# Block weights requested one block ahead, and a quarter of the modulation products moved into the mixers' merge

## The chip, the cores and the metric

The kernel runs on one core of a Trainium2 chip. A core has engines that run beside each other, each with its own instruction stream that it takes strictly in order: TensorE (PE in the profile, its weight loads PEld), VectorE (DVE), ScalarE (ACT), GpSimd (POOL) and SyncE (SP), which here only issues DMAs. They meet at semaphores. The metric is the device time of one execution in microseconds, as the median of the runs.

## The reference, cut to what matters

Two transformer-like layers act on 640 tokens (128 context, 512 latent) of width 1024. The conditioning vectors (one for the context, one for the latents) give nine modulation rows a layer:

```
mods = (silu(cond) @ w_mod[l] + b_mod[l]).reshape(Bc, 9, 1, 1024)
pre(x, s) = rmsnorm(x) * g_pre * (1 + mods[3s+1]) + mods[3s]
f = swiglu(pre(x, 0), w_ffn_gu[l, 0], w_ffn_dn[l, 0]);  x = x + 0.5 * mods[2] * rmsnorm(f) * g_post
m = token_mix(pre(x, 1), ...);                          x = x +       mods[5] * rmsnorm(m) * g_post
f = swiglu(pre(x, 2), w_ffn_gu[l, 1], w_ffn_dn[l, 1]);  x = x + 0.5 * mods[8] * rmsnorm(f) * g_post
swiglu(h) = (silu(h @ Wg) * (h @ Wu)) @ Wd              # 1024 -> 2816 -> 1024
```

`token_mix` ends in a merge: for each of 8 slices c of the width, four branch outputs are multiplied by sigmoid gates `sigmoid(h @ w_gate + b_gate)` and added, and then one projection `w_o` follows. All is float32.

## The kernel before, in words

Tokens lie along the free dimension (two halves of 320 columns), features on the 128 partitions. A float32 operand is split into a rounded part (`wh`, cast by ACT, line 219) and the rest (`wl`, subtracted by DVE, line 220), and each product is three matmuls. Every weight tile thus goes through SP (load into `raw`), ACT and DVE before PE can use it. `advance` does the split some units ahead of use and `fetch` (line 174) issues the loads: it loads until three units of the plan are ahead of the split. The `raw` tiles have three buffers.

Order of work: FFN, mixer, FFN of layer 0, then the same for layer 1. I call the four FFNs FFN1 to FFN4. An FFN's 22 hidden tiles go in four parts of 5, 5, 6 and 6. After each of the first three parts come eight `down` tasks that multiply the part by `w_dn`; POOL adds their results into DRAM (`d_f`, an accumulating DMA). The tiles of parts 1 to 3 (but the last two) are `block` tasks (line 629): a block computes gate and up of one hidden tile with seven half-size products in place of eight, on sums of weights and sums of inputs. Its weights are four pieces of one pair of loads (`raw` for gate, `ru` for up): `b`, `t`, `u` and `4`. The sums are made by three additions on POOL (lines 207 to 209, into the one buffer `wt` and in place into `ru`) when piece `b` is split, and a fourth (line 214) after it. A plan counts each piece as one unit, so `fetch` asks for a block's pair of loads when piece `u` of the block before it is about to be split. There are 15 blocks in each FFN.

The modulation rows are 2 x 9 x 8 = 144 chunks of 128 features. 16 of them are made at the start; the other 128 are made by DVE on the side: a chunk loads 512 KB of `w_mod` (tile `wm`, two buffers, line 340, issued by SP) and takes two products with the conditionings `sc` (line 352), one for each. I call them dots. `room` and `rooms` (line 795) set how many chunks stand in each task of an FFN; `todo` (line 1516) says which FFN makes which rows: 48, 32, 40 and 8 chunks in FFN1 to FFN4. `sc` is kept in DRAM (`d_sc`) and loaded again by each FFN (`cond_silu`). The mixers make none. Engines take their streams in order, so a load that waits in SP's stream holds all loads behind it, and a dot that waits for its `wm` holds DVE's splits behind it.

Of the kernel before, what the change touches and what calls it, by code (L numbers as in the profile page):

```python
# [20 lines left out]
KC = 8  # L21
# [59 lines left out]
class Kernel:  # L81
# [9 lines left out]
    def setup(self):  # L91
        tc, nc, ctx, a = self.tc, self.nc, self.ctx, self.a
        pool = lambda name, bufs, **kw: ctx.enter_context(tc.tile_pool(name=name, bufs=bufs, **kw))
        self.const = pool("const", 1)
        self.slots = pool("slots", 1)
        self.wp = pool("wp", 3)
        self.tp = pool("tp", 4)
        self.psum = pool("psum", 4, space=bass.MemoryType.PSUM)
        self.dram = pool("dram", 1, space=bass.MemoryType.DRAM)

        c = self.const
        self.ones = c.tile([P, P], F32, name="ones")
        nc.vector.memset(self.ones, 1.0)
        self.ident = c.tile([P, P], F32, name="ident")
        make_identity(nc, self.ident)
        self.rsb = c.tile([P, 2], F32, name="rsb")
        for i in range(2):
            nc.vector.memset(self.rsb[:, i:i + 1], (0.5 + 0.5 * i) * LN2 * (127.0 - 0.0430))
        self.eps = c.tile([P, 1], F32, name="eps")
        nc.vector.memset(self.eps, EPS)  # L110
        self.par, self.mod, self.co = [], [], []
        for l in range(DEPTH):
            pt = c.tile([P, C_N], F32, name=f"par{l}")
            nc.scalar.dma_start(pt, a["params"][l])
# [6 lines left out]
        self.d_sc = self.dram.tile([P, 2, D], F32, name="d_sc")  # L121
# [52 lines left out]

    def fetch(self, small):
        st = self.streams[small]
        while st["dma"] < min(st["limit"], st["split"] + (2 if small else 3)):
            ap = st["plan"][st["dma"]]
            if isinstance(ap, Piece):
# [6 lines left out]
                st["raw"].append(ap)  # L186
                st["dma"] += 1
                continue
            r = self.unit_tile(small, ap.shape[-1], F32, "raw")
            self.nc.sync.dma_start(r, ap)  # L190
            st["raw"].append(r)
            st["dma"] += 1

    def make_piece(self, p):
# [8 lines left out]
            self.split(h, lo, g[:, two])  # L203
            return h, lo
        if p.kind == "b":
            t = e["t"] = self.fp.tile([P, 2 * HK], F32, tag="wt", name=self.nm("wt"))
            add(t[:, one], g[:, one], u[:, one])
            add(t[:, two], t[:, one], u[:, two])
            add(u[:, one], u[:, one], u[:, two])
        h = self.unit_tile(False, 2 * HK, F32R, "wh")  # L210
        lo = self.unit_tile(False, 2 * HK, F32R, "wl")
        self.split(h, lo, {"b": g, "t": e["t"], "u": u}[p.kind])
        if p.kind == "b":
            add(g[:, two], g[:, two], e["t"][:, two])
        return h, lo

    def split(self, h, lo, src):

# [104 lines left out]
            pass  # L323


    def cond_silu(self):

        self.sc = self.fp.tile([P, 2, D], F32, tag="sc", name=self.nm("sc"))
        self.nc.sync.dma_start(self.sc, self.d_sc)

    def mods(self, todo, bufs=2):

        nc, a = self.nc, self.a
        loads = []

        def load(i):
            if i < len(todo):
                l, s, c = todo[i]
                wm = self.fp.tile([P, D], F32, tag="wm", name=self.nm("wm"), bufs=bufs)
                nc.sync.dma_start(wm, a["w_mod"][l, s * KC + c])  # L340
                loads.append(wm)

        for i in range(bufs - 1):
            load(i)
        yield
        for i, (l, s, c) in enumerate(todo):
            load(i + bufs - 1)
            wm = loads.pop(0)
            ch = s * KC + c
            for j in range(2):  # L350
                junk = self.t6().bitcast(BF16)[:, :D]
                nc.vector.tensor_tensor_reduce(  # L352
                    junk, wm, self.sc[:, j, :], 0.5, self.par[l][:, C_BMOD + ch:C_BMOD + ch + 1],
                    ALU.mult, ALU.add, self.mod[l][:, ch, j:j + 1])
            if c == KC - 1:
                self.section_done(l, s)
            yield

    def section_done(self, l, s):
        nc = self.nc  # L360
# [205 lines left out]
    def ffn(self, l, st, mod_todo, first=False):  # L566
# [6 lines left out]
        def begin():  # L573
            self.ph = ExitStack()
            self.fp = self.ph.enter_context(self.tc.tile_pool(name=self.nm("ffn"), bufs=1))
            self.side = None
            if mod_todo:
                self.cond_silu()
                self.side = self.mods(mod_todo)
                next(self.side)  # L580
            S["act"] = None
# [211 lines left out]


        room = {"gate": 1.4, "up": 1.4, "down": 1.0, "block": 1.0}
        rooms = [room.get(t.name, 0.0) * (0.5 if t.name == "down" and i < before else 1.0) for i, t in enumerate(mid)]
        done, n = 0.0, 0
        for t, x in zip(mid, rooms):
            done += x
# [17 lines left out]
    def mixer(self, l):  # L817
# [244 lines left out]

        def gate(c, i):
            def fn(w):
                ps = self.ps()
                self.proj(ps, w, KC, self.h)
                G[c, i] = t = self.t6()
                act.activation(two(t), ps[:, :, :HW], AF.Tanh, scale=0.5,
                               bias=self.bg[:, l, i * KC + c:i * KC + c + 1])
# [317 lines left out]
    def build(self):  # L1387
# [6 lines left out]
        def start():  # L1394
# [25 lines left out]
            sc = sp.tile([P, 2, D], F32, name="sc")  # L1420
            pcs = []
            for j in range(2):
                pcs.append(self.ps())
# [77 lines left out]
            def hook(k):  # L1501
# [10 lines left out]
                    hi(k + 2)  # L1512
                if 0 <= k + 1 < KC:
                    lo(k + 1)
                if k == KC - 1:
                    nc.sync.dma_start(self.d_sc, sc)

            hook(-3)
            hook(-2)
            for f in subs:  # L1520
# [2 lines left out]
            self.first_hook = hook  # L1523

        sec = lambda l, r: [(l, s, c) for s in r for c in range(KC)]
        todo = {(0, 0): sec(0, range(2, 8)), (0, 2): sec(0, (8,)) + sec(1, range(0, 3)), (1, 0): sec(1, range(3, 8)),
                (1, 2): sec(1, (8,))}
        nop = lambda: None
        tasks = [Task("start", start)]
        prev = None  # L1530
# [148 lines left out]
```

## Time and profile before

| what | before |
|---|---|
| median of 3 runs | 3316.44 us (3313.45 to 3317.76) |
| profiled execution | 3314.38 us, its span 3312.0 us |
| PE busy | 3069.6 us (93%) |
| DVE busy | 2341.4 us (71%) |
| ACT busy | 1392.3 us (42%) |
| POOL busy | 1092.2 us (33%) |
| DMA | 438.69 MB, 132 GB/s over the span |

The span runs from the first to the last instruction of the program; the 2.4 us to the execution's own time lie outside it. PE is the engine with most work, so time is lost where PE stands idle, and the profile is read by what ended its idle time. "A <- B" means that A's wait was ended by B.

### The profile page before, as it was taken

The numbers are of one execution on the slowest core, as the hardware profiler recorded it, in microseconds if no ns is written. First come the engines' busy times: TensorE is split into PE (matmuls) and PEld (weight loads), VectorE is DVE, ScalarE is ACT, GpSimd is POOL, SyncE is SP. The second block draws the span as 40 slices with busy tenths as digits, with TensorE's granted clock in tenths as the row PEclk, the third lists the DMA queues.
The fourth block names the chain that finished last, engine by engine and source line by source line (L and its number), as shares of the span: only waits on it lengthen the run. The fifth ranks groups of instructions, "written<-read, shape, count | busy, mean of one in ns | idle before, by whom it ended". The sixth has DMA issues, their size and how long they took to land.

```text
span 3312.0 us, 51402 instructions
## 1 busy us (share of the span) xinstructions
PE 3069.6 (93%) x20268; PEld 3001.9 (91%) x20268; DVE 2341.4 (71%) x3336; ACT 1392.3 (42%) x2407; POOL 1092.2 (33%) x856
## 2 busy tenths in 40 slices
PE   7898999899999979989989989988999999899997
PEld 6898988899999979989979889888999999899997
DVE  8877877876653487787787878688666435866666
ACT  4243345444432354343454333454444324543443
POOL 3244244510011243353343352445000113444243
PEclk9899999999999989999999999999999999999999
DMA  5436554411122345436545445533111224434344
GB/s 198 174 131 188 155 181 134 149 58 67 62 83 93 134 146 172 143 122 182 182 156 172 133 154 169 197 122 127 64 64 51 96 90 159 142 136 132 87 132 162
DMA packets 140933, 438.69 MB, mean 132 GB/s; under 512 B 16914, under 2 KB 34130, under 8 KB 139156
## 3 DMA queue, kind: packets, MB, share of 16 engines
q1 hardware_dynamic: 120100, 356.59, 31.5%
q0 software_dynamic: 20304, 78.66, 8.7%
q8 instruction: 159, 2.61, 0.3%
q14 instruction: 82, 0.67, 0.1%
q10 hardware_dynamic: 288, 0.17, 0.0%
HBM read 381.70 MB, written 53.64 MB: 131 GB/s over the span
## 4 chain that ended last, share of the span: by engine, by line
PE 56%; DVE 13%; ACT 4%; issue 3%; DMA 2%; POOL 1%; DVEq 0%; SPq 0%; ACTq 0%; POOLq 0%
PE ps L288 37%; PE ps L642 14%; DVE wl L220 4%; ACT wh L219 1%; PE ps L269 1%; PE ps L271 1%; PE ps L270 1%; DVE slotD L424 1%; DVE t L352 1%; DMA ru<-in_w_gu 1%; DVE slotB L424 1%; DVE W L1211 1%; PE ps L1202 1%; DVE act L220 1%; DMA raw<-in_w_dn 1%
## 5 line engine op out<-in xcount | busy, mean ns | idle before, releaser
L220 DVE TENSOR_TENSOR wl<-raw,wh 128x1024 fp32r<-128x1024 f32 (+3 forms) x525 | 632.0, 1205 | 371.4 <-ACT wh L219 363.1
L288 PE MATMUL ps<-act,wh 128*128 128x320 f32 x2816 | 571.1, 314 | 32.9 <-ACT act L219 19.4
L219 ACT CAST wh<-raw 128x1024 fp32r<-128x1024 f32 (+3 forms) x525 | 481.1, 919 | 153.5 <-PE ps L288 61.1
L642 PE MATMUL ps<-s,wh 128*128 128x320 f32 x1920 | 453.6, 315 | 46.3 <-ACT ps L649 36.6
L288 PEld LDWEIGHTS ps<-act,wh 128*128 128x128 f32 x2816 | 459.7, 191 | 39.3 <-ACT act L219 22.3
L352 DVE CUSTOM_DVE_ANT_0 t<-wm,sc,par 128x1024 bf16<-128x1024 f32 x256 | 373.4, 1495 | 24.4 <-DMA wm<-in_w_mod 24.0
L642 PEld LDWEIGHTS ps<-s,wh 128*128 128x128 f32 x1920 | 329.2, 189 | 63.7 <-ACT ps L649 52.3
L288 PE MATMUL ps<-slotA,wh 128*128 128x320 f32 x1312 | 366.4, 317 | 13.7 <-ACT wh L219 11.2
L288 PE MATMUL ps<-slotA,wl 128*128 128x320 f32 x1312 | 363.1, 314 | 7.2 <-DVE wl L220 7.0
L288 PE MATMUL ps<-slotD,wh 128*128 128x320 f32 x1312 | 352.9, 317 | 15.4 <-DVE slotD L1490 12.6
L288 PE MATMUL ps<-slotB,wh 128*128 128x320 f32 x1312 | 362.0, 314 | 3.1 <-DVE slotB L481 1.6
L288 PE MATMUL ps<-slotC,wh 128*128 128x320 f32 x1312 | 353.1, 317 | 7.4 <-ACT wh L219 3.1
L288 PE MATMUL ps<-act,wl 128*128 128x320 f32 x1408 | 356.6, 312 | 3.3 <-DVE wl L220 3.3
L642 PE MATMUL ps<-s,wl 128*128 128x320 f32 x960 | 298.8, 311 | 2.1 <-DVE wl L220 2.1
L288 PEld LDWEIGHTS ps<-slotA,wh 128*128 128x128 f32 x1312 | 238.8, 192 | 16.8 <-ACT wh L219 12.2
L288 PEld LDWEIGHTS ps<-slotD,wh 128*128 128x128 f32 x1312 | 236.9, 193 | 18.3 <-DVE slotD L1490 14.0
L288 PEld LDWEIGHTS ps<-act,wl 128*128 128x128 f32 x1408 | 248.7, 192 | 4.1 <-DVE wl L220 3.8
L288 PEld LDWEIGHTS ps<-slotA,wl 128*128 128x128 f32 x1312 | 239.0, 192 | 11.3 <-DVE wl L220 10.2
L288 PEld LDWEIGHTS ps<-slotC,wh 128*128 128x128 f32 x1312 | 237.1, 193 | 9.5 <-ACT wh L219 3.4
L288 PEld LDWEIGHTS ps<-slotB,wh 128*128 128x128 f32 x1312 | 238.9, 192 | 4.4 <-DVE slotB L481 2.2
L288 PE MATMUL ps<-slotC,wl 128*128 128x320 f32 x960 | 240.2, 316 | 2.0 <-DVE wl L220 1.8
L778 ACT COPY s<-ps 128x640 f32<-128x640 f32 x96 | 66.6, 694 | 298.6 <-issue 169.2
(340 smaller groups left out, 6466.0 us busy)
## 6 DMA issues: line engine op xcount, KB each, us to landing
raw<-in_w_gu SPq DMA_DIRECT2D x162, 512.0 KB, 4.2
wm<-in_w_mod SPq DMA_DIRECT2D x144, 512.0 KB, 4.3
raw<-in_w_dn SPq DMA_DIRECT2D x96, 384.0 KB, 3.3
raw<-in_w_gate SPq DMA_DIRECT2D x64, 512.0 KB, 3.5
d_f<-s POOLq DMA_DIRECT2D x96, 320.0 KB, 4.9
ru<-in_w_gu SPq DMA_DIRECT2D x60, 512.0 KB, 5.2
raw<-in_w_in SPq DMA_DIRECT2D x44, 512.0 KB, 3.4
raw<-in_w_dn SPq DMA_DIRECT2D x64, 320.0 KB, 2.9
```

The source lines that it names most:

```text
L219: self.nc.scalar.copy(h, src)
L220: self.nc.vector.tensor_sub(lo, src, h.bitcast(F32))
L269: nc.tensor.matmul(out, sh, mh, start=(k == 0), stop=False)
L270: nc.tensor.matmul(out, sh, ml, start=False, stop=False)
L271: nc.tensor.matmul(out, sl, mh, start=False, stop=(k == n - 1))
L288: nc.tensor.matmul(ps[:, hf, :HW], st[:, ws], m[:, k0 + k, hf * HW:(hf + 1) * HW], start=(first and k == 0 and i == 0), stop=(last and k = ...
L352: nc.vector.tensor_tensor_reduce(junk, wm, self.sc[:, j, :], 0.5, self.par[l][:, C_BMOD + ch:C_BMOD + ch + 1], ALU.mult, ALU.add, self.mod ...
L424: nc.vector.scalar_tensor_tensor(x, t, gain, x, op0=ALU.mult, op1=ALU.add)
L642: nc.tensor.matmul(o, w[x][:, ws], a[y][:, k, :], start=(new and k == 0 and i == 0), stop=(k == n - 1 and i == 2), skip_group_check=not new)
L778: nc.scalar.copy(t.rearrange("p (a b) -> p a b", a=2), ps[:, :, :HW])
L1202: nc.tensor.transpose(pv[:, o:o + P], pt[qi][:, j * P:(j + 1) * P], self.ident)
L1211: dve.tensor_sub(lo, src, h.bitcast(F32))
```

## The change

1. `fetch` no longer counts pieces. It counts `raw` tiles held (at most three) and up-weights in waiting (at most two), so that a block's pair of loads is issued as soon as the pair before the last has been split. The three additions are a function `sums`, called for the next block after piece `u`.
2. The chunks of modulation rows 6 and 7 (those of the second FFN of a layer) move from the FFNs into the mixer of the same layer: in the merge, each `gate(c, 1)` and `gate(c, 2)` loads one chunk into one new buffer `self.wm` ahead of its projection and places its two dots behind it. That is 16 chunks a mixer. The FFNs keep 32, 28, 28 and 8.
3. `sc` stays on chip; the four loads of 1 MB and the store go. `wm` in the FFNs has three buffers in place of two.
4. The chip memory for it comes from the DMA descriptor ring of POOL, which is given 4096 bytes a partition.

```
 def fetch(self, small):
-    while st["dma"] < min(st["limit"], st["split"] + (2 if small else 3)):
+    while st["dma"] < st["limit"]:
         ap = st["plan"][st["dma"]]
+        piece = isinstance(ap, Piece)
+        held = sum(not isinstance(r, Piece) or r.kind == "4" for r in st["raw"])
+        if not (piece and ap.kind != "b"):
+            if held >= (2 if small else 3):
+                return
+            if piece and sum(isinstance(r, Piece) and r.kind == "u" for r in st["raw"]) >= 2:
+                return
...
 def make_piece(self, p):
         if p.kind == "b":
-            t = e["t"] = self.fp.tile([P, 2 * HK], F32, tag="wt", name=self.nm("wt"))
-            add(t[:, one], g[:, one], u[:, one])
-            add(t[:, two], t[:, one], u[:, two])
-            add(u[:, one], u[:, one], u[:, two])
+            self.sums(p)
...
+        if p.kind == "u":
+            for q in self.streams[False]["raw"]:
+                if isinstance(q, Piece) and q.kind == "b":
+                    self.sums(q)
...
-    def mods(self, todo, bufs=2):
+    def mods(self, todo, bufs=3):
...
         def gate(c, i):
             def fn(w):
+                todo = [(l, 6 + i - 1, c)] if i in (1, 2) else []
+                for t in todo:
+                    self.load_mod(self.wm, *t)
                 ps = self.ps()
                 self.proj(ps, w, KC, self.h)
+                for t in todo:
+                    self.dots(self.wm, *t)
...
-        todo = {(0, 0): sec(0, range(2, 8)), (0, 2): sec(0, (8,)) + sec(1, range(0, 3)), (1, 0): sec(1, range(3, 8)),
-                (1, 2): sec(1, (8,))}
+        todo = {(0, 0): sec(0, range(2, 6)), (0, 2): sec(0, (8,)) + sec(1, (0, 1)) + half[:4],
+                (1, 0): half[4:] + sec(1, range(3, 6)), (1, 2): sec(1, (8,))}
...
-    nc = _bacc.Bacc("TRN2", target_bir_lowering=False, num_devices=1)
+    nc = _bacc.Bacc("TRN2", target_bir_lowering=False, num_devices=1,
+                     dynamic_dma_scratch_size=4096)
```

PE's and ACT's streams are the same instruction for instruction. Three places show what moves on the others. First SP's stream where part 2 of FFN2 begins: `raw` and `ru` with `in_w_gu` are a block's pair, `in_w_dn` is a down weight, `wm` a chunk. Before:

```order
355 L340 DMA wm_13379<-in_w_mod 128x1024
356 L190 DMA raw_13385<-in_w_dn 128x640
357 L340 DMA wm_13425<-in_w_mod 128x1024
358 L184 DMA raw_13431<-in_w_gu 128x1024
359 L185 DMA ru_13432<-in_w_gu 128x1024
360 L340 DMA wm_13473<-in_w_mod 128x1024
361 L340 DMA wm_13517<-in_w_mod 128x1024
362 L340 DMA wm_13566<-in_w_mod 128x1024
363 L340 DMA wm_13610<-in_w_mod 128x1024
364 L184 DMA raw_13616<-in_w_gu 128x1024
365 L185 DMA ru_13617<-in_w_gu 128x1024
```

and of the change:

```order
351 L367 DMA wm_13348<-in_w_mod 128x1024
352 L199 DMA raw_13354<-in_w_dn 128x640
353 L367 DMA wm_13394<-in_w_mod 128x1024
354 L194 DMA raw_13400<-in_w_gu 128x1024
355 L195 DMA ru_13401<-in_w_gu 128x1024
356 L194 DMA raw_13442<-in_w_gu 128x1024
357 L195 DMA ru_13443<-in_w_gu 128x1024
358 L367 DMA wm_13484<-in_w_mod 128x1024
359 L367 DMA wm_13533<-in_w_mod 128x1024
360 L367 DMA wm_13577<-in_w_mod 128x1024
361 L194 DMA raw_13591<-in_w_gu 128x1024
```

The second block's pair stood behind four chunk loads; it now stands ahead of them.

Second, DVE's stream at the start of the merge of layer 0 (`ps` to `sa` is the spatial gating's output, `br` its split, `swl` a branch weight's split, the ISA rows with `wm` are dots). Before:

```order
1040 L220 TENSOR_TENSOR wl_9279<-raw_9060,wh_9278 128x1024
1041 L1340 SCALAR_TENSOR_TENSOR sa_5560<-ps_9288,par_86,t_1365_9282 64x512
...
1053 L220 TENSOR_TENSOR br_9329<-sa_5560,br_9328 128x640
1054 L220 TENSOR_TENSOR wl_9340<-raw_9219,wh_9339 128x1024
1055 L220 TENSOR_TENSOR swl_9403<-sraw_8913,swh_9402 128x256
1056 L1083 SCALAR_TENSOR_TENSOR t_1361_9274<-t_1361_9274,ps_9406 128x640
```

and of the change:

```order
975 L373 ISA t_1312_9174,mod_88<-wm,sc,par_86 128x1024
977 L373 ISA t_1313_9176,mod_88<-wm,sc,par_86 128x1024
979 L243 TENSOR_TENSOR wl_9183<-raw_8959,wh_9182 128x1024
980 L1364 SCALAR_TENSOR_TENSOR sa_5459<-ps_9192,par_86,t_1318_9186 64x512
...
992 L243 TENSOR_TENSOR br_9233<-sa_5459,br_9232 128x640
993 L243 TENSOR_TENSOR wl_9244<-raw_9118,wh_9243 128x1024
994 L373 ISA t_1328_9297,mod_88<-wm,sc,par_86 128x1024
996 L373 ISA t_1329_9299,mod_88<-wm,sc,par_86 128x1024
998 L243 TENSOR_TENSOR swl_9312<-sraw_8812,swh_9311 128x256
999 L1107 SCALAR_TENSOR_TENSOR t_1314_9178<-t_1314_9178,ps_9315 128x640
```

Two dots stand ahead of the spatial gating's output, and two more between its split and that of a branch weight.

Third, POOL's stream around the same part 2 of FFN2 (the additions of the first and second block). Before:

```order
320 L209 TENSOR_TENSOR ru_13432<-ru_13432 128x512
321 L214 TENSOR_TENSOR raw_13431<-raw_13431,wt_13523 128x512
322 L782 DMA d_f<-s_1990_13563 128x640
323 L782 DMA d_f<-s_1997_13607 128x640
324 L207 TENSOR_TENSOR wt_13687<-raw_13616,ru_13617 128x512
```

and of the change:

```order
320 L238 TENSOR_TENSOR ru_13401<-ru_13401 128x512
321 L220 TENSOR_TENSOR raw_13400<-raw_13400,wt_13490 128x512
322 L801 DMA d_f<-s_1966_13530 128x640
323 L801 DMA d_f<-s_1973_13574 128x640
324 L236 TENSOR_TENSOR wt_13587<-raw_13442,ru_13443 128x512
```

The call of `sums` has moved in the code, but nothing has moved in POOL's stream.

## Rows read from the trace of the kernel before

**Rows 1.** The page's head and PE's line: busy us, share, instructions.

```profile
span 3312.0 us, 51402 instructions
PE 3069.6 (93%) x20268; PEld 3001.9 (91%) x20268; DVE 2341.4 (71%) x3336; ACT 1392.3 (42%) x2407; POOL 1092.2 (33%) x856
```

**Rows 2.** Windows: first down to last block of FFN1 to FFN4, busy by engine.

```profile
core 0: us, PE busy (x) PEld busy (x) DVE busy (x) ACT busy (x) POOL busy (x), PEclk, DMA share, GB/s
128.20:476.00 347.80, 311.29 (x2022) 302.78 (x2021) 275.50 (x366) 129.26 (x203) 137.53 (x87) 0.97 0.49 155
1269.90:1594.30 324.40, 306.22 (x2020) 299.37 (x2019) 249.03 (x329) 128.99 (x203) 130.73 (x86) 0.99 0.49 153
1767.50:2110.10 342.60, 310.21 (x2018) 302.08 (x2017) 266.54 (x359) 129.00 (x203) 131.64 (x86) 0.98 0.50 157
2904.50:3219.20 314.70, 301.58 (x2022) 296.33 (x2021) 192.22 (x233) 129.37 (x203) 121.29 (x87) 1.00 0.40 118
```

**Rows 3.** The same stretches, DVE's line 352 alone: four instructions a chunk.

```profile
128.20:476.00 347.80, 117.88 (x159) 0.97 0.49 155
1269.90:1594.30 324.40, 90.44 (x127) 0.99 0.49 153
1767.50:2110.10 342.60, 115.52 (x157) 0.98 0.50 157
2904.50:3219.20 314.70, 25.11 (x32) 1.00 0.40 118
```

**Rows 4.** Who waited for whom: us in total, times, longest us; SPq is SP's queue.

```profile
SPq L340 <- DVE mod L352: 539.4, 92, 14.7
POOL wt L207 <- DMA ru<-in_w_gu: 64.5, 8, 9.8
POOL wt L207 <- DVE wl L220: 43.9, 28, 3.2
DVE t L352 <- DMA wm<-in_w_mod: 24.0, 16, 3.8
```

**Rows 5.** Windows: FFN2's downs before part 2, its part 2, and FFN4's part 2.

```profile
1377.30:1412.50 35.20, 35.20 (x241) 35.15 (x241) 28.07 (x38) 11.78 (x17) 11.76 (x10) 1.00 0.83 228
1412.50:1499.40 86.90, 78.49 (x507) 75.63 (x506) 68.52 (x90) 36.25 (x59) 40.17 (x23) 0.98 0.37 123
3044.60:3124.20 79.60, 75.85 (x507) 74.01 (x506) 56.51 (x70) 36.44 (x59) 35.22 (x23) 1.00 0.27 82
```

**Rows 6.** Timelines at that start of part 2: start us, us, instruction, idle before.

```profile
1396.20 19.09 SPq L340 DMA_DIRECT2D wm<-in_w_mod  x4
1415.39 0.42 SPq L184 DMA_DIRECT2D raw<-in_w_gu  x1
1424.01 1.04 ACT L219 CAST wh<-raw 128x1024 fp32r<-128x1024 f32 x1 [3.78 <-DMA raw<-in_w_gu]
1426.77 0.41 PE L642 MATMUL ps<-s,wh 128*128 128x320 f32 x1 [3.48 <-DVE t L659]
```

**Rows 7.** Window: the merge of layer 0 from its second gate to the last branch.

```profile
966.00:1117.00 151.00, 151.00 (x1030) 150.78 (x1030) 59.36 (x82) 40.94 (x63) 19.39 (x9) 1.00 0.32 105
```

**Rows 8.** Line 352: duration ns min/median/max of the 256 dots, first and last start.

```profile
L352 DVE CUSTOM_DVE_ANT_0 t<-wm,sc,par x256: 1269/1280/2650, 86.9 to 3192.4; 128x1024 bf16<-128x1024 f32 x128
```

**Rows 9.** Timelines of DVE and PE at the start of that merge.

```profile
964.22 1.23 DVE L220 TENSOR_TENSOR wl<-raw,wh 128x1024 fp32r<-128x1024 f32 x1 [1.17 <-ACT wh L219]
965.37 4.15 DVE L1340 SCALAR_TENSOR_TENSOR sa<-ps,par,t 64x512 f32<-64x512 f32 x8
975.68 0.42 DVE L220 TENSOR_TENSOR swl<-sraw,swh 128x256 fp32r<-128x256 f32 x1
974.87 0.45 PE L288 MATMUL ps<-W,swh 128*128 128x320 f32 x2
```

**Rows 10.** POOL's timeline behind FFN2's last block, and landing of the chunk loads.

```profile
1608.05 0.54 POOL L600 DMA_DIRECT2D slotC<-d_f  x1 [4.22 <-DMA slotD<-d_x]
wm<-in_w_mod SPq DMA_DIRECT2D x144, 512.0 KB, 4.3
```

More of the change, by code (lines that the diff above doesn't have):

```diff
@@ L120, in setup @@
             nc.vector.tensor_scalar_mul(self.bg[:, l, :], self.par[l][:, C_BGATE:C_BGATE + 32], 0.5)
-        self.d_sc = self.dram.tile([P, 2, D], F32, name="d_sc")
+        self.sc = c.tile([P, 2, D], F32, name="sc")
+        self.wm = c.tile([P, D], F32, name="wm")
         self.d_x = self.dram.tile([P, KC, T], F32, name="d_x")
@@ L176, in fetch @@
         st = self.streams[small]
-        while st["dma"] < min(st["limit"], st["split"] + (2 if small else 3)):
+        while st["dma"] < st["limit"]:
             ap = st["plan"][st["dma"]]
-            if isinstance(ap, Piece):
+            piece = isinstance(ap, Piece)
[5 more added lines that the diff above has]
+                    return
+            if piece:
                 if ap.kind == "b":
@@ L185, in fetch @@
                     self.nc.sync.dma_start(e["u"], ap.up)
[L186 to L190, printed above, removed]
+                r = ap
+            else:
+                r = self.unit_tile(small, ap.shape[-1], F32, "raw")
+                self.nc.sync.dma_start(r, ap)
             st["raw"].append(r)
@@ L214, in make_piece, with sums @@
             add(g[:, two], g[:, two], e["t"][:, two])
+        if p.kind == "u":
+            for q in self.streams[False]["raw"]:
+                if isinstance(q, Piece) and q.kind == "b":
+                    self.sums(q)
         return h, lo
+    def sums(self, p):
+        e = p.env
+        if "t" in e:
+            return
+        g, u = e["g"], e["u"]
+        one, two = slice(0, HK), slice(HK, 2 * HK)
+        add = self.nc.gpsimd.tensor_add
+        t = e["t"] = self.fp.tile([P, 2 * HK], F32, tag="wt", name=self.nm("wt"))
+        add(t[:, one], g[:, one], u[:, one])
+        add(t[:, two], t[:, one], u[:, two])
+        add(u[:, one], u[:, one], u[:, two])
     def split(self, h, lo, src):
@@ L323, in rms_r @@
             pass
-    def cond_silu(self):
-        self.sc = self.fp.tile([P, 2, D], F32, tag="sc", name=self.nm("sc"))
-        self.nc.sync.dma_start(self.sc, self.d_sc)
-    def mods(self, todo, bufs=2):
-        nc, a = self.nc, self.a
+    def mods(self, todo, bufs=3):
         loads = []
@@ L337, in load @@
             if i < len(todo):
[L338 to L341, printed above, removed]
+                loads.append(self.fp.tile([P, D], F32, tag="wm", name=self.nm("wm"), bufs=bufs))
+                self.load_mod(loads[-1], *todo[i])
         for i in range(bufs - 1):
@@ L345, in mods, with load_mod, dots @@
         yield
-        for i, (l, s, c) in enumerate(todo):
+        for i, t in enumerate(todo):
             load(i + bufs - 1)
[L348 to L356, printed above, removed]
-            yield
+            self.dots(loads.pop(0), *t)
+            yield
+    def load_mod(self, wm, l, s, c):
+        self.nc.sync.dma_start(wm, self.a["w_mod"][l, s * KC + c])
+    def dots(self, wm, l, s, c):
+        ch = s * KC + c
+        for j in range(2):
+            junk = self.t6().bitcast(BF16)[:, :D]
+            self.nc.vector.tensor_tensor_reduce(
+                junk, wm, self.sc[:, j, :], 0.5, self.par[l][:, C_BMOD + ch:C_BMOD + ch + 1],
+                ALU.mult, ALU.add, self.mod[l][:, ch, j:j + 1])
+        if c == KC - 1:
+            self.section_done(l, s)
     def section_done(self, l, s):
@@ L577, in begin @@
             if mod_todo:
-                self.cond_silu()
                 self.side = self.mods(mod_todo)
@@ L795, in ffn @@
         room = {"gate": 1.4, "up": 1.4, "down": 1.0, "block": 1.0}
-        rooms = [room.get(t.name, 0.0) * (0.5 if t.name == "down" and i < before else 1.0) for i, t in enumerate(mid)]
+        rooms = [room.get(t.name, 0.0) * (0.3 if t.name == "down" and i < before else 1.0) for i, t in enumerate(mid)]
         done, n = 0.0, 0
@@ L1419, in start @@
             nc.vector.tensor_mul(cf, cf, th)
-            sc = sp.tile([P, 2, D], F32, name="sc")
+            sc = self.sc
             pcs = []
@@ L1514, in hook @@
                     lo(k + 1)
-                if k == KC - 1:
-                    nc.sync.dma_start(self.d_sc, sc)
             hook(-3)
@@ L1525, in build @@
         sec = lambda l, r: [(l, s, c) for s in r for c in range(KC)]
-        todo = {(0, 0): sec(0, range(2, 8)), (0, 2): sec(0, (8,)) + sec(1, range(0, 3)), (1, 0): sec(1, range(3, 8)),
-                (1, 2): sec(1, (8,))}
+        half = sec(1, (2,))
+        todo = {(0, 0): sec(0, range(2, 6)), (0, 2): sec(0, (8,)) + sec(1, (0, 1)) + half[:4],
+                (1, 0): half[4:] + sec(1, range(3, 6)), (1, 2): sec(1, (8,))}
         nop = lambda: None
```

## The prediction

> **What bounds the kernel now.** I read the page first. PE has 3069.6 us of work in a span of 3312.0 [rows 1], so 242 us at most can be won by filling its gaps, and DVE, ACT and POOL have less to do. The question is in which stage the gaps are and what DVE has to do there. So next I took windows of the same stretch of all four FFNs, from the first down matmul to the end of the last block [rows 2]. PE has the same work in each of them (some 2020 matmuls), ACT too, yet they last 347.8, 324.4, 342.6 and 314.7 us. What differs is DVE: 275.5, 249.0, 266.5 and 192.2 us busy. The same windows for line 352 alone say why [rows 3]: 159, 127, 157 and 32 instructions. A dot is two instructions and a chunk two dots, so the stretches hold 40, 32, 40 and 8 chunks. The side work that DVE does for the modulation is what stretches an FFN, and not in proportion. From 8 to 32 chunks it costs 9.7 us, 0.40 us a chunk. From 32 to 40 it costs 18.2 us in FFN3 (2.3 a chunk) and 23.4 in FFN1 (2.9).
>
> The waits and the timelines say how. A chunk load has two buffers and can be issued only when a dot has freed one: SP stands 539.4 us on that [rows 4], and what is behind it in its stream stands too. At the start of part 2 of FFN2, four chunk loads hold SP for 19.09 us up to 1415.3, and the second block's pair is issued only then [rows 6]. The rest is a chain: ACT idles 3.78 us for that `raw` and starts the cast at 1424.01, DVE's split and then its line 659 come late behind ACT, and PE idles 3.48 us until 1426.77 [rows 6]. POOL waits at line 207 for `ru`, 8 times and 64.5 us in all [rows 4]. Part 2 of FFN2 takes 86.9 us where that of FFN4, with hardly a chunk, takes 79.6 [rows 5].
>
> **The change part by part.** *Fewer chunks in the FFNs.* 16 go from each layer: FFN1 has 32, FFN2 28, FFN3 28, FFN4 8. Of FFN1's 48, 40 fell in the stretch of rows 3 and 8 before it, where the plan had put 11: DVE lagged by three. The new plan puts 7 of 32 before it, so 25 to 28 fall in the stretch; I take 26. By 314.7 + 0.40 x (chunks - 8), FFN1's stretch becomes 322.0 (gain 25.8), FFN2's and FFN3's 322.8 (gains 1.6 and 19.8), and FFN4's stays. That is 47.2 us. The least: FFN1 and FFN3 only come down to FFN2's 324.4, 41.6 us less what a plan in other places may cost. The most: all three come down to FFN4's 314.7, 33.1 + 9.7 + 27.9 = 70.7 us, which nothing in this profile allows to exceed.
>
> *Pairs requested earlier.* In SP's new order the second block's pair stands ahead of the chunk loads. So the case of rows 6 goes: FFN2's part 2 may lose its 7.3 us over FFN4's [rows 5]. Then FFN2's point of the line is no longer 324.4 but 317.1, 0.10 us a chunk, and the three FFNs gain up to 6 us more each, 18 in all. Zero is the other end, if the pair then waits for a buffer or the engines of the DMA. I take the middle, 9 us.
>
> *The additions called earlier.* I cost this at nothing. POOL's stream is the same before and after, so they can only start earlier if what they wait for comes earlier. In steady state that is the one buffer `wt`, freed by a DVE split (28 waits [rows 4]), and that stays. The 8 waits for `ru` belong to the pair loads, counted above.
>
> *Three `wm` buffers, `sc` kept.* The third buffer lets a chunk load go out one chunk earlier; it is a part of what makes the line hold, and I count no more for it. The four 1 MB loads stand where FFNs begin, beside the heads; no wait of PE names them: zero.
>
> *The dots in the merge.* A merge has 16 chunks, 32 dots. A dot takes 1.28 us in the median, up to 2.65 beside a POOL instruction [rows 8], so 41 us of DVE by the median in 151 us, where DVE is busy 59.4 and PE never idles [rows 7]. PE runs a gate in 48 matmuls and a branch in 12 or 24; at 151.0 / 1030 = 0.147 us each, a gate and its branch take 8.8 or 10.6 us, and DVE has 59.36 / 16 = 3.7 us of work there. Two dots fit, and the weights that DVE splits there are needed a gate later. The exception is the start. The first two dots stand ahead of the split at 964.22, before which DVE idled 1.17 us [rows 9]: 2.56 less 1.17, so the spatial gating's output, begun at 965.37, comes up to 1.4 us late; PE stands right behind it. The next two stand ahead of the split that ended at 976.10, and PE needs that weight 12 matmuls after 974.87, at 976.63 [rows 9]: 0.5 us of slack for 1.4 + 2.56. So PE loses about 3.5 us a merge, 7 us for two. Bounds: nothing, if half of it hides in DVE's idle time; 5.5 us a merge if the second two run beside POOL at 2.3 us.
>
> *The smaller ring.* POOL's transfers are already held to a number in flight: behind FFN2's last block POOL issues eight loads of `d_f`, one of `d_x` and eight of `d_f`, and the last of these waits 4.22 us for the landing of the `d_x`, eight before it [rows 10]; its data is wanted only in the second half of the tail. I cost the ring at zero, with up to 10 us at the high end should it hold POOL sooner.
>
> The Trainium skill, "SBUF — State Buffer", section "SBUF size: 192, 224, or 256?", books 16 KiB a partition for the descriptors of POOL's DMAs; it gives no price for less, and no row of before shows the ring full. If a quarter of the ring meant a quarter of the transfers in flight, two in place of eight, the sum would move toward the high end of the range and no further.
>
> The sum: 47.2 + 9 - 7 = 49 us. The profiled execution took 3314.4 us, 2.4 of them outside the span, which stay: 3265 us. It lies 2.1 us under the median of the three runs, so I set the time at 3267 us.
>
> **The rivals.** *A, the loads collide.* Nothing is loaded less in the downs: the second pair, 1 MB, now falls into a stretch where the DMA engines are busy 0.83 of the time [rows 5], ahead of three chunk loads. DVE then waits for its chunks, and as it goes in order, the next block's splits wait with it. For it: DVE waits for chunk loads already, 16 times and up to 3.8 us [rows 4]. Against it: with three buffers a load has two downs to land in, not one. If each of the nine part starts in FFN1 to FFN3 loses such a 3.8 us, 34 us go back: 3301 us.
>
> On this the Trainium skill speaks against the change: "DMA: Bandwidth & Descriptors", section "Issuing engines are not separate DMA queues", has all DMAs run on the same 16 engines and interleave, so a load brought forward slows the others. The trace does not contradict it; by that rule alone the result would be rival A's.
>
> *B, the merge pays it back.* The slower side. In the merge there is one `wm` buffer: a load can go out only after the last chunk's dots, and DVE stands until it lands. A chunk load lands 4.3 us after its issue [rows 10]. If half of the 32 chunks show PE that landing and the dots, 6.9 us, the price is 110 us, the sum 3316 - 56 + 110 = 3370 us. It decides from 56 / 32 = 1.75 us a chunk. Against it: the free 4 to 6 us in each pair, and that a load goes out most of a pair ahead of its dots.
>
> *C, the FFNs lose all their stretch.* With pairs in time, chunks cost nothing below DVE's limit: 70.7 us from above and no loss in the merge: 3246 us. Against it: FFN4 has 8 chunks, these have 26 to 28.
>
> **How the numbers follow.** My forecast has 0.66 (3253 to 3282), A 0.16, B 0.08, C 0.10. The range reaches from C to A, 3246 to 3301. Faster, by over 0.2% (about what a measurement of this kernel can tell, 6.6 us), are my case, C and most of A: 0.88. A might end within 0.2% at 0.04. Slower is B: 0.08.
>
> **What would show it.** In the changed profile the stretches of rows 2 should be near 322 for the first three, with 26 to 28 chunks; POOL's wait for `ru` under 15 us, the second pair issued before the downs end, and no PE idle of 3.5 us at the start of a part. The merge should last 154 to 155 us in place of 151, with one wait of PE on `br` or `swl` at its start and none later. Waits of DVE for `wm` over 24 us in the FFNs speak for A; waits of PE in the middle of the merge for B. I am wrong if the stretches of FFN1 and FFN3 stay above 330 with the chunks gone: then DVE's load is not what stretches them.

## The result, and the profile after

The changed kernel takes 3268.4 us (median; 3263.9 to 3271.4) beside 3317.1 us (3313.5 to 3322.4) of the kernel before on the same chip: 0.9851 of it, with a 95% interval of 0.9833 to 0.9869. The prediction was 3267 us.

The page's head and PE's line, which answer to [rows 1]:

```profile
span 3269.4 us, 51367 instructions
PE 3057.0 (94%) x20268; PEld 2990.7 (91%) x20268; DVE 2364.8 (72%) x3336; ACT 1392.4 (43%) x2407; POOL 1088.8 (33%) x856
```

The span is 42.6 us shorter (the profiled execution was the longest of its four, 3271.4 us). No engine has less to do to speak of; PE's gaps went from 242 to 212 us, and its own time fell by 12.6 us, at the same number of matmuls. Of PE's waits, the one for ACT's copy of a result in a block (line 652 before, 671 now) fell most, from 27.1 to 10.4 us:

```profile
PE ps L642 <- ACT t L652: 27.1, 28, 3.3
PE ps L661 <- ACT t L671: 10.4, 23, 1.1
```

Where the time went is seen in the four stretches of [rows 2] and their dots [rows 3] (windows of the changed kernel: us, busy by engine with instructions, then clock, DMA share, GB/s):

```profile
130.23:451.94 321.71, 304.77 (x2022) 298.20 (x2021) 235.90 (x301) 126.74 (x199) 131.23 (x87) 0.99 0.47 142
1247.84:1567.75 319.91, 304.57 (x2022) 297.80 (x2021) 244.41 (x313) 128.81 (x203) 133.10 (x86) 0.99 0.48 147
1742.12:2062.07 319.95, 303.11 (x2022) 296.19 (x2021) 245.72 (x314) 128.76 (x203) 132.24 (x86) 1.00 0.48 147
2858.93:3174.67 315.74, 302.97 (x2022) 297.78 (x2021) 195.57 (x233) 129.66 (x203) 120.96 (x86) 0.99 0.41 116
```

and the dots alone (DVE's line 373, which was 352):

```profile
130.23:451.94 321.71, 75.07 (x103) 0.99 0.47 142
1247.84:1567.75 319.91, 82.59 (x111) 0.99 0.48 147
```

The stretches became 26.1, 4.5 and 22.7 us shorter and FFN4's 1.0 longer, 52.2 in all. They hold 26, 28 and 28 chunks (103 and 111 instructions, four a chunk). Outside them the span grew by 9.6 us. The waits that answer to [rows 4] (who waited for whom: us, times, longest):

```profile
SPq L367 <- DVE mod L373: 157.0, 46, 8.8
POOL wt L236 <- DVE wl L243: 49.6, 36, 1.7
DVE t L373 <- DMA wm<-in_w_mod: 11.2, 10, 2.4
```

SP stands 157 us for a dot in place of 539; POOL's wait for `ru` is no longer listed; DVE waits less for chunks, not more. The start of FFN2's part 2, which answers to [rows 6], in SP's queue:

```profile
1375.64 0.33 SPq L194 DMA_DIRECT2D raw<-in_w_gu  x1
1376.02 0.50 SPq L195 DMA_DIRECT2D ru<-in_w_gu  x1
1376.57 14.74 SPq L367 DMA_DIRECT2D wm<-in_w_mod  x3
```

The second block's pair goes out at 1375.64, 15 us before the part begins at 1390.8; it was 2.9 us after it. The chunk loads still hold SP for 14.74 us, but behind the pair. PE's longest wait in that part is now this one (it was 3.48 us):

```profile
1402.14 0.41 PE L661 MATMUL ps<-s,wh 128*128 128x320 f32 x1 [1.27 <-DVE t L678]
```

In each merge, which answers to [rows 7, 9], PE now waits twice, both at the start (the first merge; DVE's and PE's timelines):

```profile
938.81 1.28 DVE L373 CUSTOM_DVE_ANT_0 t<-wm,sc,par 128x1024 bf16<-128x1024 f32 x1
941.15 4.13 DVE L1364 SCALAR_TENSOR_TENSOR sa<-ps,par,t 64x512 f32<-64x512 f32 x8
952.65 1.28 DVE L373 CUSTOM_DVE_ANT_0 t<-wm,sc,par 128x1024 bf16<-128x1024 f32 x1
953.86 0.42 DVE L243 TENSOR_TENSOR swl<-sraw,swh 128x256 fp32r<-128x256 f32 x1
949.37 0.56 PE L311 MATMUL ps<-br,swh 128*128 128x320 f32 x2 [0.81 <-ACT br L242]
954.34 0.56 PE L311 MATMUL ps<-W,swl 128*128 128x320 f32 x2 [1.49 <-DVE swl L243]
```

The dots at 938.81 delay the spatial gating's output, and the split `br` comes 0.81 us late; the next two delay the split of the branch weight by 1.49 us. No wait of PE stands behind the other 28 dots of the merge.

### The profile page after: what moved, and what is told of

Its sections match the earlier page's. It is cut to its first block, busy times and chain, and to the rows that moved or that the text cites. A ratio compares the mean times of both kernels' runs of the same rounds, so it can differ in the third digit from the quotient of the medians.

```text
span 3269.4 us, 51367 instructions
## 1 busy us (share of the span) xinstructions
PE 3057.0 (94%) x20268; PEld 2990.7 (91%) x20268; DVE 2364.8 (72%) x3336; ACT 1392.4 (43%) x2407; POOL 1088.8 (33%) x856
## 5 line engine op out<-in xcount | busy, mean ns | idle before, releaser
L243 DVE TENSOR_TENSOR wl<-raw,wh 128x1024 fp32r<-128x1024 f32 (+3 forms) x525 | 645.5, 1232 | 421.2 <-ACT wh L242 413.0
L373 DVE CUSTOM_DVE_ANT_0 t<-wm,sc,par 128x1024 bf16<-128x1024 f32 x256 | 374.4, 1498 | 11.3 <-DMA wm<-in_w_mod 11.2
```

The lines of the kernel that those rows point to most:

```text
L243: self.nc.vector.tensor_sub(lo, src, h.bitcast(F32))
L373: self.nc.vector.tensor_tensor_reduce(junk, wm, self.sc[:, j, :], 0.5, self.par[l][:, C_BMOD + ch:C_BMOD + ch + 1], ALU.mult, ALU.add, sel ...
```

## The experiments

All times were taken beside the kernel before on the same chip. The table has the ratio to it with its 95% interval, and the four stretches, from windows of one profiled execution as in [rows 2].

| kernel | time us | ratio | FFN1 | FFN2 | FFN3 | FFN4 |
|---|---|---|---|---|---|---|
| before | 3317 | 1 | 347.8 | 324.4 | 342.6 | 314.7 |
| the change | 3268.4 | 0.9851 (0.9833 to 0.9869) | 321.7 | 319.9 | 320.0 | 315.7 |
| chunks moved, pairs as before | 3271.7 | 0.9863 (0.9843 to 0.9882) | 320.0 | 321.8 | 323.8 | 315.2 |
| pairs earlier, chunks as before | 3301.4 | 0.9954 (0.9938 to 0.9969) | 339.3 | 321.9 | 336.3 | 314.5 |
| additions not called earlier | 3269.2 | 0.9853 (0.9837 to 0.9870) | 321.2 | 319.8 | 319.5 | 315.4 |
| small ring alone | 3318.9 | 1.0007 (0.9997 to 1.0017) | 349.9 | 325.8 | 340.6 | 316.1 |
| two `wm` buffers | 3269.4 | 0.9853 (0.9840 to 0.9867) | 321.4 | 320.2 | 322.0 | 315.6 |
| merge's first dots moved | 3262.9 | 0.9828 (0.9814 to 0.9841) | 321.3 | 320.0 | 320.5 | 315.6 |
| 28 more chunks in the fills | 3272.7 | 0.9857 (0.9844 to 0.9871) | 317.9 | 317.5 | 321.3 | 312.2 |
| 20 more, in quiet gates | 3261.1 | 0.9828 (0.9815 to 0.9842) | 318.0 | 320.1 | 321.4 | 316.2 |
| thin dots | 3237.5 | 0.9750 (0.9736 to 0.9764) | 309.1 | 313.5 | 312.3 | 313.7 |
| one load an FFN | 3267.1 | 0.9838 (0.9825 to 0.9852) | 321.3 | 320.0 | 320.5 | 315.5 |
| before with one load | 3291.6 | 0.9920 (0.9906 to 0.9933) | 334.9 | 319.6 | 333.6 | 316.1 |
| before with thin dots | 3236.1 | 0.9756 (0.9743 to 0.9769) | 311.7 | 314.3 | 316.3 | 313.6 |

The kernel before and the one with the small ring alone run the same instructions, and their stretches differ by 2.1, 1.4, 2.0 and 1.4 us. A difference of up to 2 us in a single stretch tells nothing by itself.

### The chunks without the pairs, and the pairs without the chunks

The first has the new `todo`, the dots in the merge, `sc` kept and the small ring, but the old `fetch`, the old additions and two `wm` buffers. The second is the other part alone:

```
 first:   + gate: self.load_mod(self.wm, *t) ... self.dots(self.wm, *t);  new todo, rooms;  sc kept
 second:  + fetch counts held raw tiles and up-weights;  sums() called after piece u
```

> The chunks move into the merge, sc stays on chip and the ring is small, but pairs are requested as before and wm keeps two buffers. My theory (the chunk count is what stretches the FFNs): the stretches of FFN1 to FFN3 fall to about 322, 323 and 323 us, the merges lose 2.6 us each, the whole gains 40 us, ratio 0.988. Rival (late pairs are what stretches them, the chunks only happen to be there): the pairs stay late, at most 20 us are gained, ratio 0.994 or more.

> Only the request of the pairs and the place of the call of the additions change; chunks, buffers, sc and ring are those of before. My theory: a gain of 9 to 18 us (ratio 0.9946 to 0.9973), FFN1 and FFN3 stay above 335 us with their 40 chunks. Rival (late pairs are the cause): 30 us or more, ratio 0.991 or less, and all three stretches near 322. Rival (loads collide): no gain or a loss, with more waits of DVE for wm.

Both theories held: chunks alone gave 45.5 us (40 expected), pairs alone 15.8 (9 to 18), and FFN1 and FFN3 stayed above 335 us in the second. Together they gave 48.7 us, not 61. With the chunks moved, the pairs are worth some 3 us (3271.7 to 3268.4), and the intervals of the two ratios overlap. Why, is seen in the first kernel at the start of FFN2's part 2 (SP's queue and PE's wait):

```profile
1371.49 16.40 SPq L346 DMA_DIRECT2D wm<-in_w_mod  x3
1387.94 0.42 SPq L186 DMA_DIRECT2D raw<-in_w_gu  x1
1398.03 0.42 PE L640 MATMUL ps<-s,wh 128*128 128x320 f32 x1 [0.58 <-DVE t L657]
```

The second pair is still held behind chunk loads, and is issued 0.6 us after its part began (at 1387.37, by the first matmul of line 640). But PE then loses 0.58 us, where it lost 3.48 at 2.9 us [rows 6]. With three chunk loads in the queue in place of four the pair came 2.3 us sooner, and that was nearly enough.

### The additions, the ring, the third buffer

```
 additions:  - if p.kind == "u": ... self.sums(q)      (from the changed kernel)
 ring:       + dynamic_dma_scratch_size=4096           (to the kernel before)
 buffers:    - def mods(self, todo, bufs=3)   + bufs=2 (in the changed kernel)
```

> The changed kernel, with the three additions called only at piece b as before. The streams of all five engines are the same as in the changed kernel. My theory: the same time as the changed kernel, ratio to before 0.985. Rival (the earlier call matters, by the semaphores it waits on): 5 us or more slower than the changed kernel, ratio 0.987 or more.

> The kernel before with a ring of 4096 bytes a partition and nothing else. My theory: no difference, ratio 0.999 to 1.001, and POOL's loads behind a last block issue at the same intervals. Rival (the small ring holds POOL's DMAs back): 3 to 10 us slower, ratio 1.001 to 1.003, with longer waits of POOL behind the last blocks.

> The changed kernel with two wm buffers in the FFNs, as before the change, in place of three. Theory: with 28 chunks an FFN and the pairs ahead of them, SyncE waits for a dot but nothing that it holds is late, so the third buffer is worth nothing: within 4 us of the changed kernel, 0.984 to 0.986 of before. Rival: the third buffer is what lets a load land in time; without it VectorE waits at every part's start, some 4 us nine times: 3290 to 3305 us, 0.992 or more.

None of the three can be told from its neighbour (0.9853, 1.0007, 0.9853). With the additions called early or late, all engines run the same instructions in the same order. The ring's smaller size costs at most 0.2%. With two buffers the three chunk loads at FFN2's part 2 hold SP 14.27 us in place of 14.74, behind the pair as before.

### The start of the merge

```
-todo = [(l, 6 + i - 1, c)] if i in (1, 2) else []
+todo = [(l, 6 + i - 1, c)] if i in (1, 2) and c else []
+if c == KC - 1 and i in (0, 3):
+    todo = [(l, 6 if i == 0 else 7, 0)]
```

> The changed kernel with the four dots at the start of each merge (chunk 0 of rows 6 and 7) moved to the last two gates of the fill ahead of it, where the tensor engine never stood and VectorE was busy 52 of 90 us. Theory: the 2.6 us a merge that the changed kernel loses at its first gate (1.0 us on br, 1.65 us on swl) come only from those four dots, so both merges lose nothing there: about 5 us less than the changed kernel, 3263 to 3264 us, 0.983 to 0.984 of before. Rival: the loss is handed on to the next branch or comes back in the fill: 3268 us, 0.985.

No wait of PE is left in the window of the merge. The two mixers (from FFN1's stretch to FFN2's, and from FFN3's to FFN4's) are 3.6 and 3.2 us shorter than in the changed kernel, and all that lies outside the stretches sums to 1982.7 us, as before the change (1982.5; 1992.1 in the changed kernel). So the theory holds: the four dots were the loss. By the median this version is 5.5 us faster than the changed kernel (3262.9 and 3268.4 us), though the intervals of the two ratios overlap.

### Dots or loads

Two kernels take the two halves of a chunk apart. In thin dots, the FFNs' dots run over one column in place of 1024, all loads stay; with one load, an FFN's dots all run on its first `wm`.

```
 thin dots:  - junk, wm, self.sc[:, j, :], 0.5     + junk[:, :1], wm[:, :1], self.sc[:, j, :1], 0.5
 one load:   - if i < len(todo): load              + if i < 1: load
```

> The changed kernel with the FFNs' dots taken over one column in place of 1024 (their sums are left out); loads, waits and instruction order stay. VectorE has about 70 us less to do in each of FFN1 to FFN3. Theory: what the chunks still cost in an FFN is VectorE's time, so the first three stretches (321.7, 320.1, 320.0 us) come down to FFN4's 315.7 or below, by 0.22 us a chunk: 15 to 25 us less than the changed kernel, 3244 to 3254 us, 0.978 to 0.981 of before. Rival: it is the transfers of the chunks and the places of their loads in SyncE's stream; then at most 3 us go, 3265 us or more, 0.984 or more.

> The counterpart: the changed kernel with one chunk load an FFN and all of the FFN's dots on that one tile (the rows made in the FFNs are then wrong in value); the dots keep their number, place and length, 92 loads of 512 KB and their waits are gone. Theory (VectorE's time): within 3 us of the changed kernel, 3265 to 3271 us, 0.984 to 0.986. Rival (transfers and the loads' place): the 15 to 25 us go here, 0.978 to 0.981.

Without DVE's time 33 us go (0.9851 to 0.9750), more than I expected; without 48 MB of loads nothing goes that can be told (0.9851 to 0.9838). What the chunks still cost is the time of their dots, not their loads. With thin dots POOL's instructions are shorter too (33.55 us in place of 40.32 in the windows below), and no run tells POOL's share from DVE's. Where, is seen by setting the downs before FFN2's part 2 and that part beside each other. The changed kernel:

```profile
1355.60:1390.80 35.20, 35.20 (x243) 35.20 (x241) 26.85 (x37) 11.77 (x17) 11.80 (x10) 1.00 0.84 243
1390.80:1473.10 82.30, 76.44 (x505) 73.81 (x504) 69.69 (x88) 36.15 (x59) 40.32 (x23) 1.00 0.37 117
```

and with thin dots:

```profile
1337.00:1372.20 35.20, 35.20 (x242) 35.20 (x241) 15.35 (x39) 11.77 (x17) 11.73 (x10) 1.00 0.89 251
1372.27:1451.00 78.73, 75.37 (x505) 73.79 (x504) 54.49 (x87) 36.65 (x59) 33.55 (x23) 1.00 0.38 119
```

The eight downs take 35.20 us with six chunks' dots at full length or over one column: there chunks are free. The same holds for the second and third eight downs of all four FFNs in these two kernels (35.20 and 42.24 us). The part's six blocks take 82.3 or 78.7: chunks cost where they stand in blocks. One such place, in the second block of that part, step by step (timelines of DVE, ACT and PE of the changed kernel):

```profile
1404.12 1.27 DVE L373 CUSTOM_DVE_ANT_0 t<-wm,sc,par 128x1024 bf16<-128x1024 f32 x1
1405.32 2.30 DVE L373 CUSTOM_DVE_ANT_0 t<-wm,sc,par 128x1024 bf16<-128x1024 f32 x1
1410.27 1.07 DVE L690 TENSOR_TENSOR t<-t,t 128x320 f32<-128x320 f32 x1
1411.37 0.73 ACT L242 CAST act<-t 128x640 fp32r<-128x640 f32 x1 [3.24 <-DVE t L690]
1412.00 0.42 ACT L671 COPY t<-ps 128x320 f32<-128x320 f32 x1
1412.47 0.42 PE L661 MATMUL ps<-slotA,wh 128*128 128x320 f32 x1 [0.49 <-ACT t L671]
```

The two dots (the second beside an addition of POOL, 2.30 us) push the block's last product on DVE, line 690, back; ACT's cast of it waits 3.24 us, and behind that cast in ACT's stream stands the copy of line 671, for which PE waits. Over the kernel PE waits 23 times and 10.4 us for that copy; with thin dots that wait is not listed. It is half of the 21 us by which PE's gaps shrink with thin dots (from 212.4 to 191.4 us); PE's own time falls by another 16.6 us (3057.0 to 3040.4) at the same number of matmuls.

The same two cuts in the kernel before:

> The kernel before the change with one chunk load an FFN and all of the FFN's dots on that tile (the rows made in the FFNs are wrong in value): no chunk load holds SyncE's queue any more, and VectorE keeps all 48, 32, 40 and 8 chunks. Theory (VectorE's time is most of what the chunks cost, the held loads the smaller part, as the earlier pairs alone gave 16 us): 12 to 20 us less than before, 0.994 to 0.996, and FFN1 and FFN3 still near 340 and 337 us. Rival (what stretches FFN1 and FFN3 from 32 to 40 chunks is SyncE held by chunk loads): 40 us or more go, 0.988 or less.

> The kernel before the change with the FFNs' dots taken over one column in place of 1024 (their sums are left out); all loads and all places stay. Theory (VectorE's time): FFN1 to FFN3 come down to 312 to 318 us, some 70 to 80 us less than before, 0.976 to 0.979. Rival (the place of the loads in SyncE's queue counts by itself, and dots shorter by 1.2 us free a buffer only that much sooner): a part's first block stays late, 25 us or more of it remain, 0.983 or more.

Without the dots' time the kernel before is as fast as the changed kernel without it (3236.1 and 3237.5 us), with all its chunk loads and the old order of the pairs: the theory. The cut is not quite clean, since shorter dots also free the buffers sooner: four chunk loads still hold SP for 17.15 us at FFN2's part 2, but the second pair goes out 1.4 us ahead of the part, where it was 2.9 us behind its start. Without the held loads 25 us went, more than I expected of it and less than the rival wanted. The two causes overlap: the two gains, 80.7 and 25.2 us, cannot be added. That a late pair costs most where DVE has no room to catch up would explain it, but no run shows this by itself.

### Still fewer chunks in the FFNs

The mixer places its `gate(c, 0)` and `gate(c, 3)` between the steps of the attention; these stretches are the fills.

```
 28 more:  gate(c, 0) and gate(c, 3), c < 7: one chunk each of rows 5 and (1, 0) or (1, 8)
 20 more:  gate(c, 3), c < 7, and gate(c, 0), c = 1, 3, 5 alone; both with the merge's first dots moved
```

> A version meant to beat both: as the one before, and 28 more chunks (14 a mixer) moved out of the FFNs into the fill gates of the attention, one a gate, two dots behind each projection. FFN1 to FFN4 keep 26, 20, 22 and 0 chunks in place of 32, 28, 28 and 8. Theory: the remaining slope, 0.22 us a chunk between 8 and 28 chunks, times 28 is 6 us off the FFNs, and the fills take the dots for nothing, as VectorE was busy 60 to 64% of them and the tensor engine over 99%: 3256 to 3259 us, 0.982. Rival: in the fills a dot of 1.28 us stands ahead of a softmax step for which ScalarE and then the tensor engine wait; 28 chunks at 0.5 us or more pay it all back: 3268 us or more, 0.985 or more.

> The version with 28 more chunks in the fills, cut to 20: none in the gates at which that one lost time (the first, where VectorE's stream was full, 3.4 us late on swl and 2.8 on br; and the third, fifth and seventh of the first kind, where dots stood ahead of the splits of the attention's weights, line 1239, 1.3 to 1.5 us each). FFN1 to FFN4 keep 25, 23, 23 and 5 chunks. Theory: those places alone cost the 17 us that its two mixers lost, the other gates are free, and the FFNs give back 0.3 us a chunk, as the thin dots showed (28 us for 92 chunks): 6 us less than the version with the merge's start alone, 0.980 to 0.9815 of before. Rival: the dots in the quiet gates also come back, as later softmax steps or a lower clock: 0.983 or more.

The first fell to its rival. Its FFNs gave back 8.5 us, but its mixers took more. PE's waits in the first mixer's fills (who waited for whom: us, times, longest):

```profile
PE ps L292 <- DVE W L1239: 3.6, 3, 1.3
PE ps L311 <- DVE swl L243: 3.0, 1, 3.0
PE ps L311 <- ACT br L242: 2.6, 1, 2.6
```

and DVE at the first of the three waits for `W`:

```profile
728.07 1.28 DVE L373 CUSTOM_DVE_ANT_0 t<-wm,sc,par 128x1024 bf16<-128x1024 f32 x1
729.27 1.28 DVE L373 CUSTOM_DVE_ANT_0 t<-wm,sc,par 128x1024 bf16<-128x1024 f32 x1
730.60 1.55 DVE L1239 TENSOR_TENSOR W<-ps,W 128x768 fp32r<-128x768 f32 x2
```

DVE had room in the fill (62 of 80 us busy), but not at that gate. The second version left those four gates of a mixer out, and none of the three waits grew there: the quiet gates are free. Yet it is no faster than the version with the merge's start alone (both 0.9828), so its forecast of 6 us missed. Its FFNs, with 25, 23, 23 and 5 chunks, gained 3.2 us in FFN1 and nothing in the others. FFN1's gain lies in its first eight downs (41.6 to 38.3 us). In FFN2 ten dots are gone, five of them from the blocks: the blocks of the first two parts became 0.7 and 0.8 us shorter, but those of the last part 1.1 us longer, with six dots in place of eight. So a price of 0.3 us a chunk was wrong. What a chunk costs depends on the place of its dots, and why the last part became longer is open. Taking all chunks out did gain: FFN4, left without any in the first version, takes 312.2 us.

## Why the prediction came out right

The sum met the median within 2 us, closer than its terms, and that is luck. The stretches fell by 52.2 us where 47.2 and 9 were forecast, and what lies outside them grew by 9.6 where 7 was forecast; the profiled spans give 42.6 us in all, the medians 48.7.

*Chunks out of the FFNs, 47.2 us.* Right in size: with that part alone the stretches fell by 27.8, 2.6 and 18.8 us, beside 25.8, 1.6 and 19.8 forecast, and 26 and 28 chunks stand in them. But the line of 0.40 us a chunk from which the forecast came is no law. The dots of the second and third downs cost nothing, those of blocks something, and not in proportion. A part of six blocks takes 78.8 us without a dot (FFN4 of the version with 28 more) and 82.3 with twelve (above). In the kernel before with one load, where no chunk load holds SP, FFN1's has fourteen and FFN3's sixteen:

```profile
286.90:370.60 83.70, 76.77 (x506) 73.88 (x505) 72.88 (x94) 35.95 (x59) 40.99 (x23) 1.00 0.25 71
1896.60:1985.60 89.00, 78.34 (x506) 75.44 (x505) 76.66 (x98) 35.92 (x59) 41.00 (x23) 0.98 0.25 67
```

The first twelve dots cost 3.5 us, the last two alone 5.3. Nor is there a price for each dot: in the changed kernel the four blocks of the last part take 53.7 us with eight dots in FFN2 and 54.2 with two in FFN4, and 52.9 with thin dots. That 26 and 28 chunks came out on the line through 8 and 32 is in part luck.

What stretched FFN1 and FFN3 beyond the line I put on loads that hold SP's queue. The runs show both causes. Without the held loads FFN1 and FFN3 of the kernel before came down by 12.9 and 9.0 us, and stayed 13.6 and 13.1 us above the changed kernel with one load (321.3 and 320.5). The old order of the pairs is not what is left: FFN2, with that order and 32 chunks, takes 319.6 us beside 320.0. Without the dots' time FFN1 and FFN3 came down by 36.1 and 26.3 us. In FFN1 10.8 of its 26.1 us came from its first eight downs, which the prediction did not look at. The change also has an edit that its description leaves out: a down of these eight counts 0.3 in place of 0.5 of a task when the chunks are shared out.

```
-        rooms = [room.get(t.name, 0.0) * (0.5 if t.name == "down" and i < before else 1.0) for i, t in enumerate(mid)]
+        rooms = [room.get(t.name, 0.0) * (0.3 if t.name == "down" and i < before else 1.0) for i, t in enumerate(mid)]
```

Thirteen dots start in them before, six after the change. By the kernel's own sums (an estimate) the plan gave them 4.3 chunks, would give 2.9 with 32 chunks at the old share, and gives 1.8 at the new one; no run has the one without the other. Their window in the kernel before:

```profile
128.20:181.00 52.80, 39.52 (x243) 38.59 (x242) 38.93 (x53) 15.14 (x22) 16.63 (x14) 0.84 0.50 178
```

in the changed kernel:

```profile
130.23:172.20 41.97, 37.55 (x242) 37.02 (x241) 24.74 (x33) 12.68 (x18) 14.30 (x12) 0.92 0.52 179
```

and with thin dots:

```profile
129.80:165.20 35.40, 35.40 (x242) 35.20 (x241) 15.51 (x30) 12.69 (x18) 12.54 (x12) 1.00 0.55 188
```

PE's two longest waits there in the kernel before:

```profile
140.28 0.90 PE L288 MATMUL ps<-act,wh 128*128 128x320 f32 x2 [4.82 <-ACT act L219]
148.41 1.44 PE L288 MATMUL ps<-act,wh 128*128 128x320 f32 x4 [6.70 <-DVE act L220]
```

the last of four dots ahead of that split on DVE, and the split:

```profile
143.01 2.54 DVE L352 CUSTOM_DVE_ANT_0 t<-wm,sc,par 128x1024 bf16<-128x1024 f32 x1
147.55 0.81 DVE L220 TENSOR_TENSOR act<-t,act 128x640 fp32r<-128x640 f32 x1
```

and the only wait in the changed kernel:

```profile
139.19 1.43 PE L311 MATMUL ps<-act,wh 128*128 128x320 f32 x4 [4.40 <-DVE act L243]
```

DVE came out of the FFN's head with dots still to do, and the splits of `act` stood behind them. With PE idle its granted clock fell (0.84, 0.92 and 1.00 in the three windows), and the same 242 matmuls took 39.5, 37.6 and 35.4 us. Around the two waits of the kernel before, where PE ran for 1.43 of 8 us, the clock stood at 0.50, the lower of its two levels (1.2 and 2.4 GHz):

```profile
138.00:146.00 8.00, 1.43 (x4) 1.03 (x4) 8.00 (x12) 0.72 (x1) 3.94 (x2) 0.50 0.44 160
```

*Earlier pairs, 9 us.* Mis-sized: 3 us on top of the moved chunks (3271.7 to 3268.4, the intervals overlap), though 16 by themselves. The prediction took FFN2's part 2 to FFN4's 79.6 us; it came to 82.3, and what is left is dots in blocks. The wait it named did go, from 3.48 to 1.27 us.

*Additions, `sc` and the third buffer, the ring: nothing.* Right for the three that were run alone or undone. `sc` was not tried by itself. The ring's high end of 10 us is not borne out: 1.0007, at most 1.0017, which is 5.6 us. The Trainium skill ("SBUF — State Buffer", section "SBUF size: 192, 224, or 256?") states the 16 KiB and no price for less; that a quarter of the ring would hold POOL was the prediction's own thought.

*The merge, 3.5 us each.* Right in place, too large in size: 0.81 and 1.49 us of waits, 2.3 in all, and mixers that are 2.0 and 2.5 us longer than before (3.6 and 3.2 us of their length went when the four dots moved). No wait of PE stands behind the dots later in the merge.

*Rival A* (loads collide): DVE's waits for chunks fell to 11.2 us, and without 92 of the loads the time is the same. The Trainium skill ("DMA: Bandwidth & Descriptors", section "Issuing engines are not separate DMA queues") states that all DMAs share the engines; that a load brought forward would cost time was the prediction's inference from it, and it has no price here. With the DMA engines 0.84 busy in the downs, DVE waits ten times for a chunk, 2.4 us at most. *Rival B* (the merge pays it back) needed 1.75 us a chunk; four of the 32 cost 4.6 us of waits together, the others none. *Rival C* (no stretch left, 3246 us) is reached only with thin dots, 3237.5 us, not with the dots in the blocks. The 70.7 us that the prediction called the most are not the most: thin dots in the kernel before took 73.6 us off the stretches and 80.7 off the time. FFN4, which it took for the floor, pays for its eight chunks too (315.6 us with them and 312.2 without, in the versions with the merge's first dots moved).

Outside the stretches 9.6 us were lost, where 7 were forecast for the merges. The mixers have 4.5 of them; the rest lies in the start, between FFN2 and FFN3, and at the end, at 1 to 2 us each, and changes from run to run as much (the first down comes at 130.2 us here, and at 128.4 in the run whose streams are the same). It is not explained further.

The runs point to one more version that was not tried: more of an FFN's chunks in its second and third downs, where twelve dots cost nothing (and sixteen in the kernel before with one load), and fewer in its blocks. Not all would fit: 28 chunks are 56 dots, 72 us of DVE at 1.28 us each. By the thin dots' stretches it would have at most 6 to 8 us each in FFN1 (behind its first downs), FFN2 and FFN3 to win.

## What to carry to other kernels

Ask of side work on a shared engine not how much there is, but what stands behind each piece in the streams: here two 1.3 us products were free in one task and cost 0.6 us in the next (the mean of six blocks), since ACT's copy stood behind a cast that waited for them. Two fixes for one stall don't add: the earlier loads were worth 16 us alone and some 3 beside the moved work, so price the second in the state that the first leaves. A line through two stages that differ in one count is good for a forecast near its points, and for nothing else: above the second point sixteen dots in a part cost 5.3 us more than fourteen, and from 28 to 23 chunks nothing was gained.

## What was not expected of the hardware

The dots slow POOL and are slowed by it. In the changed kernel none of the 154 dots that ran beside no POOL instruction took over 1.29 us, and each of the 54 that took over 1.6 us ran beside an arithmetic one of POOL. With thin dots POOL's instructions of FFN2's part 2, the same 23, take 33.55 us in place of 40.32, and one dot of the changed kernel took 3.1 us, where the median is 1.28 (line 373: minimum, median and maximum in ns):

```profile
L373 DVE CUSTOM_DVE_ANT_0 t<-wm,sc,par x256: 1271/1280/3116, 88.9 to 3147.9; 128x1024 bf16<-128x1024 f32 x128
```

And the price of a stall of PE is more than its length: in FFN1's first downs of the kernel before, where the clock was 0.84 in the mean, the matmuls took 4.1 us more (39.52 less 35.40) on top of the waits.
